# Gate and up products of three feed-forward stages by seven products of quarters

## The chip, the cores and the metric

The kernel runs on one core of a Trainium2 chip. The metric is device time in microseconds of one execution. Every engine (TensorE for matmuls, VectorE, ScalarE, GpSimd, SyncE) works through its own queue in order; semaphores tie the queues together. In the profile TensorE is PE (PEld: its weight loads), VectorE DVE, ScalarE ACT, GpSimd POOL, SyncE SP.

## The reference

Two transformer blocks over 512 tokens of 1024 float32 values. The first (attention, convolution and a mixture of experts) is not touched. The second has two layers; each has a feed-forward stage, a mixer (a pooling mixer in layer 0, MLA, a latent attention, in layer 1) and a second feed-forward stage:

```python
def swiglu(h, w_gate, w_up, w_down):
    return (jax.nn.silu(h @ w_gate) * (h @ w_up)) @ w_down
...
    for i in range(DEPTH_2):
        h = rmsnorm_2(x, ffn1_norm[i])
        x = x + FFN_HALF * swiglu(h, ffn1_w_gate[i], ffn1_w_up[i], ffn1_w_down[i])
        h = rmsnorm_2(x, mix_norm[i])
        ...
        h = rmsnorm_2(x, ffn2_norm[i])
        x = x + FFN_HALF * swiglu(h, ffn2_w_gate[i], ffn2_w_up[i], ffn2_w_down[i])
```

Gate and up are 1024 x 2816, down is 2816 x 1024. Below FFN(1,0), FFN(2,0), FFN(1,1) and FFN(2,1) are the four stages in order of time (first or second of a layer, layer); the pooling mixer stands between the first two, MLA between the last two.

## The kernel before

**Products.** A float32 product is made of three matmuls (`mm3`, L247 to L249): each operand is split into a high part (`hi`, a cast on ScalarE) and a low part (`lo`, the rest, a subtraction on VectorE), and hi x hi, hi x lo and lo x hi add up in PSUM. Stationary is a 128x128 tile of weights, moving are the tokens (transposed, `xT`, hidden values on partitions), 512 columns at a time.

**Weights.** `Weights` holds the whole program's list of weight units. SyncE fetches raw chunks of 1 MB into a ring (`wraw`); `_split` makes `whi` (L161, ScalarE) and `wlo` (L162, VectorE) of a unit of at most 128x1024. `next` hands the next unit to the products and splits ahead, two units beyond the one in use, into rings of `NU` = 4 buffers.

**A feed-forward stage** (`ffn`). A front norms the 512 tokens (X, float32, in four groups of 128): square sum on ScalarE (`junk`, L275), root on GpSimd, product `hrow` on VectorE (L282), eight transposes on TensorE into `pB` and `pC` (L294), cast `xTh` (L255) and split `xTl` (L256). The hidden width is done in 22 blocks of 128 columns, in three parts, `PARTS` = (0,8), (8,15), (15,22). A block is a gate product (24 matmuls of 512 columns: 8 slices of 1024 times 3) into one half of a two-bank PSUM tile `pA`, an up product into its other half, Silu on ScalarE (L1052), product of both on VectorE (L1054), and the split of that into `hh` (L255) and `hl` (L256). The first two blocks run on tokens 0 to 255 first and on 256 to 511 afterwards, so that TensorE can begin when two of four token groups are normed. After each part come the down products of its blocks, for the two halves of the output columns (`dh`): four accumulators, one per token group, in `pB` and `pC`, and at the end X is updated (L1103). In the last part the second half runs token group by token group, so that the next stage's front can begin with the first. There are two `pA` tiles of two banks, two `pB` and two `pC` of one bank.

**Order.** A scheduler sets the order of each engine's queue from the order of the code and from priorities (the front runs with a raised one), when the program is built. PSUM and SBUF tiles are guarded as whole tiles: an instruction that writes one half of a `pA` tile waits for a reader of the other half that comes before it in the code.

## Time and profile before

| | us |
|---|---|
| median of 3 runs (2659.57 to 2660.88) | 2659.93 |
| the profiled execution | 2662.16 |
| its span in the trace | 2660.4 |
| TensorE busy | 2554.8 (96%) |
| VectorE busy | 1046.5 (39%) |
| ScalarE busy | 735.2 (28%) |

The stages in the trace: projections, attention and experts up to about 820 us, FFN(1,0) to 1215, pooling mixer to 1244, FFN(2,0) to 1622, FFN(1,1) to 2005, MLA to 2280, FFN(2,1) to 2656. Records of matmuls overlap, since the next starts while the former drains through the array: the time from start to start is what one costs in a stream, and a window's count of matmuls gives the same. Records of weight loads lie under the matmuls. The granted clock (PEclk) is a share of full speed.

### The profile page before, as it was taken

The numbers are of one execution on the slowest core, as the hardware profiler recorded it, in microseconds if no ns is written. First come the engines' busy times: TensorE is split into PE (matmuls) and PEld (weight loads), VectorE is DVE, ScalarE is ACT, GpSimd is POOL, SyncE is SP. The second block draws the span as 40 slices with busy tenths as digits, with TensorE's granted clock in tenths as the row PEclk, the third lists the DMA queues.
The fourth block names the chain that finished last, engine by engine and source line by source line (L and its number), as shares of the span: only waits on it lengthen the run. The fifth ranks groups of instructions, "written<-read, shape, count | busy, mean of one in ns | idle before, by whom it ended". The sixth has DMA issues, their size and how long they took to land.

```text
span 2660.4 us, 28926 instructions
## 1 busy us (share of the span) xinstructions
PE 2554.8 (96%) x12006; PEld 1858.5 (70%) x12006; DVE 1046.5 (39%) x1627; ACT 735.2 (28%) x1243; POOL 90.9 (3%) x142
## 2 busy tenths in 40 slices
PE   6999889999998999998999999999999999999999
PEld 4855644333335887888887878777778777888887
DVE  5665322222225333336333334333335566533332
ACT  4333210000003322224322223222224645322221
POOL 1000200000001000001000000000001000000000
PEclk9999889999998999999999999999999999999999
DMA  7254479999996323232232322223222111122321
GB/s 266 92 178 166 164 290 420 408 416 419 418 419 217 104 87 97 86 103 83 95 96 87 94 98 94 95 79 103 79 87 80 58 58 64 64 99 76 119 76 59
DMA packets 185492, 411.90 MB, mean 155 GB/s; under 512 B 7460, under 2 KB 126784, under 8 KB 157712
## 3 DMA queue, kind: packets, MB, share of 16 engines
q1 hardware_dynamic: 183168, 403.73, 41.5%
q0 software_dynamic: 1184, 2.97, 0.3%
q10 hardware_dynamic: 1008, 3.34, 0.3%
q8 instruction: 94, 1.54, 0.2%
q14 instruction: 38, 0.31, 0.0%
HBM read 407.92 MB, written 2.10 MB: 154 GB/s over the span
## 4 chain that ended last, share of the span: by engine, by line
PE 61%; issue 30%; DVE 3%; ACT 3%; DMA 2%; POOL 2%; SPq 0%; ACTq 0%; POOLq 0%; DVEq 0%
PE pA L966 9%; PE pA L247 7%; PE pA L248 7%; PE pA L249 7%; PE pB L966 4%; PE pC L248 3%; PE pC L249 3%; PE pC L247 3%; PE pB L248 2%; PE pB L247 2%; PE pB L249 2%; PE pC L940 1%; PE ms L1397 1%; PE pC L1015 1%; PE pC L741 1%
## 5 line engine op out<-in xcount | busy, mean ns | idle before, releaser
L161 ACT CAST whi<-wraw 128x1024 fp32r<-128x1024 f32 (+2 forms) x334 | 335.9, 1011 | 1092.1 <-PE pA L248 684.8
L162 DVE TENSOR_TENSOR wlo<-wraw,whi 128x1024 fp32r<-128x1024 f32 (+2 forms) x334 | 391.9, 1177 | 479.6 <-ACT whi L161 468.1
L248 PE MATMUL pA<-xTl,whi 128*128 128x512 f32 (+1 forms) x1536 | 578.1, 377 | 1.3 <-DVE xTl L256 1.3
L249 PE MATMUL pA<-xTh,wlo 128*128 128x512 f32 (+1 forms) x1536 | 578.0, 377 | 0.0
L247 PE MATMUL pA<-xTh,whi 128*128 128x512 f32 (+1 forms) x1536 | 574.1, 381 | 3.4 <-ACT xTh L255 3.0
L247 PEld LDWEIGHTS pA<-xTh,whi 128*128 128x128 f32 x1536 | 289.7, 189 | 78.9 <-ACT sl L1052 21.9
L249 PEld LDWEIGHTS pA<-xTh,wlo 128*128 128x128 f32 x1536 | 289.8, 189 | 56.7
L248 PEld LDWEIGHTS pA<-xTl,whi 128*128 128x128 f32 x1536 | 290.2, 189 | 54.7 <-DVE xTl L256 1.7
L1054 DVE TENSOR_TENSOR sl<-pA,sl 128x512 f32<-128x512 f32 x88 | 60.9, 692 | 427.6 <-PE pA L249 427.5
L966 PE MATMUL pA<-wraw,wideh 128*64 128x512 f32 x832 | 215.9, 597 | 0.5 <-DVE wideh L949 0.5
L966 PEld LDWEIGHTS pA<-wraw,wideh 128*64 128x64 f32 x832 | 63.4, 137 | 109.3 <-issue 108.2
L247 PE MATMUL pC<-whi,hh 128*128 128x512 f32 x352 | 138.5, 393 | 0.0
L248 PE MATMUL pC<-wlo,hh 128*128 128x512 f32 x352 | 138.5, 393 | 0.0
L249 PE MATMUL pC<-whi,hl 128*128 128x512 f32 x352 | 138.4, 393 | 0.0
L247 PE MATMUL pB<-whi,hh 128*128 128x512 f32 x352 | 138.3, 393 | 0.0
L248 PE MATMUL pB<-wlo,hh 128*128 128x512 f32 x352 | 138.3, 393 | 0.0
L249 PE MATMUL pB<-whi,hl 128*128 128x512 f32 x352 | 138.1, 392 | 0.0
L966 PE MATMUL pB<-wraw,hx 128*64 128x512 f32 x320 | 100.5, 596 | 0.0
L262 POOL TENSOR_SCALAR ms<-ss 128x1 f32<-128x1 f32 x46 | 18.8, 409 | 1747.1 <-ACT junk L275 1713.5
L247 PEld LDWEIGHTS pB<-whi,hh 128*128 128x128 f32 x352 | 66.1, 188 | 15.5 <-DVE X L1103 0.7
L247 PEld LDWEIGHTS pC<-whi,hh 128*128 128x128 f32 x352 | 66.1, 188 | 14.9
L249 PEld LDWEIGHTS pB<-whi,hl 128*128 128x128 f32 x352 | 66.1, 188 | 14.8
(495 smaller groups left out, 3314.5 us busy)
## 6 DMA issues: line engine op xcount, KB each, us to landing
wraw<-in_w_up_dram SPq DMA_DIRECT2D x61, 1024.0 KB, 12.4
wraw<-in_w_gate_dram SPq DMA_DIRECT2D x43, 1024.0 KB, 12.0
wraw<-in_w_down_dram SPq DMA_DIRECT2D x40, 1024.0 KB, 10.5
wraw<-in_ffn_w_gate_dram SPq DMA_DIRECT2D x40, 1024.0 KB, 5.3
wraw<-in_ffn_w_up_dram SPq DMA_DIRECT2D x40, 1024.0 KB, 5.3
wraw<-in_ffn_w_down_dram SPq DMA_DIRECT2D x32, 1024.0 KB, 4.9
wraw<-in_w_ada_dram SPq DMA_DIRECT2D x24, 1024.0 KB, 7.8
widel<-in_w_down_dram SPq DMA_DIRECT2D x16, 1024.0 KB, 7.7
```

What stands on the lines that cost most here:

```text
L161: self.nc.scalar.copy(out=hi, in_=src)
L162: self.nc.vector.tensor_sub(lo, src, f(hi))
L247: PE.matmul(o, a[0], b[0], start=first, stop=False)
L248: PE.matmul(o, a[0], b[1], start=False, stop=False)
L249: PE.matmul(o, a[1], b[0], start=False, stop=last)
L262: G.tensor_scalar(ms, ss, 1.0 / n, EPS, op0=OP.mult, op1=OP.add)
L741: PE.matmul(o[r], Vf[:, blk, r], x, start=z == 0, stop=z == len(blks) - 1)
L940: PE.matmul(p, ohr[:, t], h[:, t, c_], start=t + z == 0, stop=t + z == T)
L966: PE.matmul(outs[dh][r], x[:, k, r], ws[e][:, j, dh * 512:(dh + 1) * 512], start=k == 0, stop=k == K - 1)
L1015: PE.matmul(p, Se[:, t * P:(t + 1) * P], ys[dh][s], start=s == 0, stop=s == 1)
L1054: V.tensor_mul(sl, a[:, 512:1024], sl)
L1397: PE.matmul(p[:, :nn], q[a][:, c_], k[b][:, :nn], start=first, stop=False)
```

## The change

`ffn_fast` takes the place of `ffn` in FFN(2,0), FFN(1,1) and FFN(2,1). The hidden width is done in 11 pairs of 256 columns, in four parts, `PAIRS`. A gate or up product of a pair is a product of 256 columns x 1024 by 1024 x 512 tokens; cut into quarters (256 in two halves of 128, 1024 in two of 512, tokens in two of 256) it is eight products of 12 matmuls of 256 tokens as it stands, and seven with sums of quarters (Winograd's form of Strassen's method). `seven` picks where: gates from pair 2, ups of pair 1 and of even pairs. The other products stay 2 x 24 matmuls of 512.

For a product by seven, `sums` puts four units in the list instead of two. `_form` makes the sums of weight quarters on VectorE (four operations of 512), and three units of 1024 and one of 512 are split. The sums of token quarters are made once in each stage by `form_sums`, from a float32 copy of the tokens (`x32`) that ScalarE writes in the front beside `xTh`. The seven results are put together on VectorE (three operations of 512 and one of 256: L1214, L1218, L1219, L1223 of the changed kernel) and a copy of 256 on ScalarE (L1210). A gate by seven takes both `pA` tiles, an up by seven the two `pB` and two `pC`; the down products of dh = 0 take `pA` tiles. Silu, the product, and the split of the hidden values act on 1024 elements at a time. `mla_tables`, which runs on the small engines inside FFN(2,0), shares some of its tiles.

```diff
@@ -119,6 +119,26 @@
+    def sums(self, c):
+        self.units.append((c, lambda v: v[:, :, 0:P], 0))
+        self.units.append((c, 0, 0))
+        self.units.append((c, 1, 0))
+        self.units.append((c, lambda v: v[:, 4:8, P:2 * P], 0))
+        self.left[c] += 4
+    def _form(self, v, which):
+        a11, a12, a21, a22 = v[:, 0:4, 0:P], v[:, 4:8, 0:P], v[:, 0:4, P:2 * P], v[:, 4:8, P:2 * P]
+        t = self.tmp.tile([P, 1024], F32, name="wsum", tag="wsum", bufs=2).rearrange("p (a b) -> p a b", b=P)
+        if which == 0:
+            self.nc.vector.tensor_add(t[:, 4:8], a21, a22)
+            self.nc.vector.tensor_sub(t[:, 0:4], t[:, 4:8], a11)
+            self.second = t[:, 0:4]
+        else:
+            self.nc.vector.tensor_sub(t[:, 0:4], a11, a21)
+            self.nc.vector.tensor_sub(t[:, 4:8], a12, self.second)
+        return t
@@ -151,7 +171,7 @@
     def _split(self, i):
         c, pick, raw = self.units[i]
-        src = pick(self.tiles[c])
+        src = self._form(self.tiles[c], pick) if isinstance(pick, int) else pick(self.tiles[c])
@@ -387,7 +407,30 @@
     PARTS = [(0, 8), (8, 15), (15, 22)]
+    PAIRS = [(0, 3), (3, 6), (6, 9), (9, 11)]
+    def seven(pr, m):
+        return pr > 1 and (m == 0 or pr % 2 == 0) or pr == 1 and m == 1
+    def plan_fast(which, i):
+        g, u, d = (I[f"ffn{which}_w_{n}_2"][i] for n in ("gate", "up", "down"))
+        for p0, p1 in PAIRS:
+            for pr in range(p0, p1):
+                for m, ap in enumerate((g, u)):
+                    c = W.chunk([(0, P, rows(ap, 0, K, 2 * pr * P, 2 * P))], (P, K, 2 * P))
+                    if seven(pr, m):
+                        W.sums(c)
+                        continue
+                    for a in range(2):
+                        W.unit(c, lambda v, a=a: v[:, :, a * P:(a + 1) * P])
+            for dh in range(2):
+                plan_cols(d[2 * p0 * P:2 * p1 * P], 2 * (p1 - p0), dh * 512, 512, 4, 2)
     def plan_ffn(which, i):
+        if (which, i) != (1, 0):
+            plan_fast(which, i)
+            return
         g, u, d = (I[f"ffn{which}_w_{n}_2"][i] for n in ("gate", "up", "down"))
@@ -1104,6 +1147,148 @@
+    def ffn_fast(pool, gain, last=False, hook=None):
+        W.tmp = pool
+        xT = pair()
+        st = ExitStack()
+        xp = st.enter_context(tc.tile_pool(name="x32", reuse_waits=RW, bufs=1))
+        x32 = xp.tile([P, K, S], F32, name="x32")
+        def put_at(t):
+            two = split_into(xT, t)
+            def put(g, m, pv):
+                two(g, m, pv)
+                A.copy(out=x32[:, g:g + m, t * P:(t + 1) * P], in_=pv)
+            return put
+        with tc.high_priority(offset=200):
+            for t in range(T):
+                transposed(norm_rows(nrms[1], X[:, t], gain), K, put_at(t))
+        nrms[0].close()
+        right = ExitStack()
+        tp = right.enter_context(tc.tile_pool(name="tsum", reuse_waits=RW, bufs=1, side="right"))
+        ts = [tp.tile([P, 4, 4, 256], F32R, name="ts" + z) for z in "hl"]
+        def form_sums():
+            b11, b12, b21, b22 = (x32[:, a:a + 4, c:c + 256] for a in (0, 4) for c in (0, 256))
+            t = [xp.tile([P, 4, 256], F32, name=n, tag=n) for n in ("tsa", "tsb")]
+            def done(i, v):
+                split(ts[0][:, i], ts[1][:, i], v)
+            V.tensor_sub(t[0], b12, b11)
+            V.tensor_sub(t[1], b22, t[0])
+            done(1, t[1])
+            done(0, t[0])
+            V.tensor_sub(t[0], b22, b12)
+            done(2, t[0])
+            V.tensor_sub(t[1], b21, t[1])
+            done(3, t[1])
+        def proj(o, w, c0, c1):
+            for k in range(K):
+                mm3(o[:, c0:c1], [x[:, k] for x in w], [x[:, k, c0:c1] for x in xT], k == 0, k == K - 1)
+        def product(o, w, k0, b):
+            for k in range(4):
+                mm3(o, [x[:, k0 + k] for x in w], [x[:, k] for x in b], k == 0, k == 3)
+        def plain(k0, c0):
+            return [x[:, k0:k0 + 4, c0:c0 + 256] for x in xT]
+        def by_seven(bk, res):
+            two = [b.rearrange("p (h n) -> p h n", h=2) for b in bk]
+            tt = [[x[:, i] for x in ts] for i in range(4)]
+            w = W.next()
+            product(two[3][:, 0], w, 0, plain(0, 0))
+            m1 = pool.tile([P, 256], F32, name="m1", tag="m1", bufs=1)
+            A.copy(out=m1, in_=two[3][:, 0])
+            product(two[0][:, 0], w, 4, plain(4, 0))
+            w = W.next()
+            product(two[0][:, 1], w, 0, tt[1])
+            V.tensor_add(res[:, 0::3], two[0], m1[:, None, :].to_broadcast([P, 2, 256]))
+            product(two[1][:, 0], w, 4, tt[0])
+            w = W.next()
+            product(two[1][:, 1], w, 0, tt[2])
+            V.tensor_add(res[:, 1:3], two[1], res[:, 3:4].to_broadcast([P, 2, 256]))
+            V.tensor_add(res[:, 3], two[1][:, 0], res[:, 2])
+            product(two[2][:, 0], w, 4, plain(4, 256))
+            w = W.next()
+            product(two[2][:, 1], w, 0, tt[3])
+            V.tensor_add(res[:, 1:3], two[2], res[:, 1:3])
+        hp = None
+        for p0, p1 in PAIRS:
+            if hook is not None and p0 > 0:
+                hook()
+                hook = None
+            hs = []
+            for pr in range(p0, p1):
+                ga = [psA(), psA()] if seven(pr, 0) else [psA()]
+                ub = [psB(), psB(), psC(), psC()] if seven(pr, 1) else [psB(), psC()]
+                gb = [a[:, c:c + 512] for a in ga for c in (0, 512)]
+                rg = pool.tile([P, 4, 256], F32, name="rg", tag="rg", bufs=1)
+                rgf = rg.rearrange("p a n -> p (a n)")
+                if pr == 0:
+                    ws = []
+                    for o in gb + ub:
+                        ws.append(W.next())
+                        proj(o, ws[-1], 0, 256)
+                    form_sums()
+                    st.close()
+                    hp = st.enter_context(tc.tile_pool(name="hid", reuse_waits=RW, bufs=3))
+                    for o, w in zip(gb, ws):
+                        proj(o, w, 256, 512)
+                elif seven(pr, 0):
+                    by_seven(gb, rg)
+                else:
+                    for o in gb:
+                        proj(o, W.next(), 0, 512)
+                A.activation(rgf, rgf if seven(pr, 0) else ga[0], AF.Silu)
+                if seven(pr, 1):
+                    ru = pool.tile([P, 4, 256], F32, name="ru", tag="ru", bufs=1)
+                    by_seven(ub, ru)
+                    V.tensor_mul(rgf, ru.rearrange("p a n -> p (a n)"), rgf)
+                else:
+                    for j, o in enumerate(ub):
+                        if pr == 0:
+                            proj(o, ws[2 + j], 256, 512)
+                        else:
+                            proj(o, W.next(), 0, 512)
+                        V.tensor_mul(rgf[:, j * 512:(j + 1) * 512], o, rgf[:, j * 512:(j + 1) * 512])
+                hh, hl = (hp.tile([P, 1024], F32R, name=n, tag=n) for n in ("hh", "hl"))
+                split(hh, hl, rgf)
+                hs.append((hh, hl))
+            n = 2 * (p1 - p0)
+            for dh in range(2):
+                a = [psA(), psA()] if dh == 0 else None
+                acc = [x[:, c:c + 512] for x in a for c in (0, 512)] if a else [psB(), psB(), psC(), psC()]
+                c_ = slice(dh * 512, (dh + 1) * 512)
+                if dh == 1 and 2 * p1 == FB:
+                    ws = [W.next() for _ in range(n // 2)]
+                    order = [(t, z) for t in range(T) for z in range(n)]
+                else:
+                    ws = []
+                    order = [(t, z) for z in range(n) for t in range(T)]
+                for t, z in order:
+                    if z // 2 == len(ws):
+                        ws.append(W.next())
+                    h0 = z % 2 * 512 + t * P
+                    mm3(acc[t], [x[:, h0:h0 + P] for x in hs[z // 2]], [x[:, z % 2] for x in ws[z // 2]],
+                        z == 0, z == n - 1)
+                    if z == n - 1:
+                        V.scalar_tensor_tensor(X[:, t, c_], acc[t], 0.5, X[:, t, c_], op0=OP.mult, op1=OP.add)
+        st.close()
+        right.close()
+        open_nrm()
...
@@ -1488,13 +1673,13 @@
         with tc.tile_pool(name="f20", reuse_waits=RW, bufs=1) as p_:
             nxt, gain = gain, load_gain(I["ffn1_norm_2"][1:2])
             mcs = []
-            ffn(p_, nxt, hook=lambda: mcs.extend(mla_tables(ml)))
+            ffn_fast(p_, nxt, hook=lambda: mcs.extend(mla_tables(ml)))
             nxt, gain = gain, load_gain(I["mix_norm_2"][1:2])
-            ffn(p_, nxt)
+            ffn_fast(p_, nxt)
-        ffn(p_, gain, last=True)
+        ffn_fast(p_, gain, last=True)
```

TensorE's queue in the second part of FFN(2,0). Before, where the up of block 10 begins (`pA_8498` is its tile, `pA_8566` that of block 11):

```order
L249 MATMUL pA_8566<-xTh_7338,wlo_8501 128x512
L247 MATMUL pA_8566<-xTh_7338,whi_8500 128x512
L247 MATMUL pA_8498<-xTh_7338,whi_8465 128x512 [waits Activation_49]
L248 MATMUL pA_8498<-xTl_7339,whi_8465 128x512
L249 MATMUL pA_8498<-xTh_7338,wlo_8466 128x512
```

After, in the gate of pair 4 (`pA_8556` holds its first two sums, `pA_8557` the other two; `whi_8523`, `whi_8566` and `whi_8596` are its second, third and fourth unit):

```order
L268 MATMUL pA_8557<-xTl_7341,whi_8566 128x256
L269 MATMUL pA_8557<-xTh_7340,wlo_8567 128x256
L267 MATMUL pA_8557<-tsh_7450,whi_8596 128x256
L267 MATMUL pA_8556<-tsh_7450,whi_8523 128x256 [waits DVE_49]
L268 MATMUL pA_8556<-tsl_7451,whi_8523 128x256
L269 MATMUL pA_8556<-tsh_7450,wlo_8524 128x256
```

Seven matmuls of the block behind, of which the last two are shown, stood in front of a wait on ScalarE's Silu. Now a whole product of the third unit and one matmul of the fourth stand in front of a wait on VectorE, inside a gate.

VectorE's queue at the same place; before, two blocks (`sl` is the product with the gate, `hl` the low part of the hidden values):

```order
L162 TENSOR_TENSOR wlo_8437<-wraw_8154,whi_8436 128x1024 [waits DMAHW0_49,PE_49,Activation_49]
L1054 TENSOR_TENSOR sl_8367<-pA_8366,sl_8367 128x512 [waits PE_49,Activation_49]
L162 TENSOR_TENSOR wlo_8466<-wraw_8220,whi_8465 128x1024 [waits DMAHW1_49,Activation_49]
L256 TENSOR_TENSOR hl_8431<-sl_8367,hh_8430 128x512 [waits Activation_49]
L162 TENSOR_TENSOR wlo_8501<-wraw_8154,whi_8500 128x1024 [waits PE_49,Activation_49]
L1054 TENSOR_TENSOR sl_8435<-pA_8434,sl_8435 128x512 [waits PE_49,Activation_49]
L162 TENSOR_TENSOR wlo_8532<-wraw_8220,whi_8531 128x1024 [waits Activation_49]
L256 TENSOR_TENSOR hl_8495<-sl_8435,hh_8494 128x512 [waits Activation_49]
```

After, the gate of pair 4 by seven (`hl_8553` belongs to pair 3, `rg` is the gate's result, `ru` the up's):

```order
L276 TENSOR_TENSOR hl_8553<-rg_8376,hh_8552 128x1024 [waits Activation_49]
L182 TENSOR_TENSOR wlo_8628<-wraw_8224,whi_8627 128x1024 [waits PE_49,Activation_49]
L1214 TENSOR_TENSOR rg_8562<-pA_8556,m1_8582 128x2x256 [waits DVE_49,PE_49]
L182 TENSOR_TENSOR wlo_8661<-wsum_8657,whi_8660 128x1024 [waits PE_49,Activation_49]
L1218 TENSOR_TENSOR rg_8562<-pA_8556,rg_8562 128x512 [waits DVE_49,PE_49]
L182 TENSOR_TENSOR wlo_8683<-wsum_8679,whi_8682 128x1024 [waits Activation_49]
L1219 TENSOR_TENSOR rg_8562<-pA_8556,rg_8562 128x256 [waits DVE_49]
L182 TENSOR_TENSOR wlo_8713<-wraw_8224,whi_8712 128x512 [waits PE_49,Activation_49]
L1223 TENSOR_TENSOR rg_8562<-pA_8557,rg_8562 128x512 [waits DVE_49]
L134 TENSOR_TENSOR wsum_8773<-wraw_8414 128x512 [waits DMAHW0_49]
L138 TENSOR_TENSOR wsum_8803<-wraw_8414 128x512
L182 TENSOR_TENSOR wlo_8744<-wraw_8414,whi_8743 128x1024 [waits PE_49,Activation_49]
```

Before, two splits of weights and two operations on hidden values take turns; now the result sums that wait on TensorE stand between splits of the units for the next products, and the forms of weights (`wsum`) are added.

ScalarE's queue at the front of FFN(1,1), from the first square sum. Before:

```order
L275 ACTIVATE junk_9746,ss_9747<-X_71 128x1024 [waits DVE_49,Pool_49]
L255 CAST xTh_9744<-pB_9755 128x4x128 [waits PE_49]
L275 ACTIVATE junk_9769,ss_9770<-X_71 128x1024 [waits DVE_49,Activation_49,Pool_49]
L255 CAST xTh_9744<-pB_9778 128x4x128 [waits PE_49]
L275 ACTIVATE junk_9792,ss_9793<-X_71 128x1024 [waits DVE_49,Activation_49,Pool_49]
L255 CAST xTh_9744<-pC_9762 128x4x128 [waits PE_49]
L161 CAST whi_9646<-wraw_9489 128x1024 [waits DMAHW6_49,PE_49]
L161 CAST whi_9650<-wraw_9556 128x1024 [waits DMAHW7_49,PE_49]
L255 CAST xTh_9744<-pB_9801 128x4x128 [waits PE_49]
L255 CAST xTh_9744<-pC_9785 128x4x128 [waits PE_49]
```

After (`x32` is the float32 copy):

```order
L295 ACTIVATE junk_10598,ss_10599<-X_71 128x1024 [waits DVE_49,Pool_49]
L295 ACTIVATE junk_10623,ss_10624<-X_71 128x1024 [waits DVE_49,Activation_49,Pool_49]
L275 CAST xTh_10592<-pB_10607 128x4x128 [waits PE_49]
L181 CAST whi_10708<-wraw_10374 128x1024 [waits DMAHW7_49,PE_49]
L275 CAST xTh_10592<-pB_10632 128x4x128 [waits PE_49]
L295 ACTIVATE junk_10648,ss_10649<-X_71 128x1024 [waits DVE_49,Activation_49,Pool_49]
L1165 COPY x32_10597<-pB_10607 128x4x128 [waits PE_49]
L275 CAST xTh_10592<-pC_10615 128x4x128
L1165 COPY x32_10597<-pB_10632 128x4x128 [waits DVE_49]
L181 CAST whi_10736<-wraw_10374 128x1024 [waits PE_49]
L1165 COPY x32_10597<-pC_10615 128x4x128 [waits DVE_49]
L275 CAST xTh_10592<-pB_10657 128x4x128 [waits PE_49]
```

The copies of `x32` stand between the casts `xTh`; each frees the PSUM tile of a transpose later than the casts alone did.

## Rows read from the trace of the kernel before

**Rows 1.** Page, part 1: busy time, share of the span, count of instructions.
```profile
PE 2554.8 (96%) x12006; PEld 1858.5 (70%) x12006; DVE 1046.5 (39%) x1627; ACT 735.2 (28%) x1243; POOL 90.9 (3%) x142
```

**Rows 2.** Windows in two feed-forward stages; columns in the first line.
```profile
core 0: us, PE busy (x) PEld busy (x) DVE busy (x) ACT busy (x) POOL busy (x), PEclk, DMA share, GB/s
...
1300.00:1350.00 50.00, 50.00 (x215) 39.89 (x215) 15.42 (x17) 13.23 (x16) 0.00 (x0) 1.00 0.27 91
1400.00:1450.00 50.00, 50.00 (x214) 39.66 (x213) 16.20 (x17) 13.62 (x18) 0.00 (x0) 1.00 0.28 95
```

**Rows 3.** Waits of TensorE, 2285 to 2660: total us, times, longest.
```profile
PE pB L294 <- DVE xTl L256: 1.0, 1, 1.0
```

**Rows 4.** Timeline of TensorE: start, duration, line, tiles, shapes; one place in consecutive blocks.
```profile
1400.74 0.73 PE L247 MATMUL pA<-xTh,whi 128*128 128x512 f32 x2
...
1411.99 0.71 PE L247 MATMUL pA<-xTh,whi 128*128 128x512 f32 x2
```

**Rows 5.** Timeline of TensorE in the halves of 256 tokens, 15 matmuls.
```profile
1253.73 0.28 PE L247 MATMUL pA<-xTh,whi 128*128 128x256 f32 x1
...
1255.39 0.28 PE L249 MATMUL pA<-xTh,wlo 128*128 128x256 f32 x1
```

**Rows 6.** Groups by line and shape: count, busy us, mean ns, idle before.
```profile
L162 DVE TENSOR_TENSOR wlo<-wraw,whi 128x1024 fp32r<-128x1024 f32 x294 | 358.8, 1224 | 461.6 <-ACT whi L161 450.3 <-PE pB L623 4.1
L161 ACT CAST whi<-wraw 128x1024 fp32r<-128x1024 f32 x294 | 306.7, 1048 | 1009.6 <-PE pA L248 639.2 <-PE pC L249 284.5 <-issue 24.4
...
L247 PEld LDWEIGHTS pA<-xTh,whi 128*128 128x128 f32 x1536 | 289.7, 189 | 78.9 <-ACT sl L1052 21.9 <-ACT xTh L255 3.9
...
L1054 DVE TENSOR_TENSOR sl<-pA,sl 128x512 f32<-128x512 f32 x88 | 60.9, 692 | 427.6 <-PE pA L249 427.5
L256 DVE TENSOR_TENSOR hl<-sl,hh 128x512 fp32r<-128x512 f32 x88 | 60.3, 685 | 0.7
L255 ACT CAST hh<-sl 128x512 fp32r<-128x512 f32 x88 | 54.7, 621 | 3.3 <-DVE sl L1054 3.3
...
L162 DVE TENSOR_TENSOR wlo<-wraw,whi 128x512 fp32r<-128x512 f32 x16 | 10.9, 680 | 0.0
```

**Rows 7.** Timeline of VectorE: back to back (1228), then inside a block (1418).
```profile
1229.63 0.68 DVE L256 TENSOR_TENSOR pll<-pB,plh 128x512 fp32r<-128x512 f32 x1
1230.22 1.28 DVE L256 TENSOR_TENSOR pll<-pC,plh 128x512 fp32r<-128x512 f32 x2
1231.42 0.68 DVE L1157 TENSOR_TENSOR X<-pB,X 128x512 f32<-128x512 f32 x1
...
1418.18 0.69 DVE L1054 TENSOR_TENSOR sl<-pA,sl 128x512 f32<-128x512 f32 x1 [5.26 <-PE pA L249]
1418.96 1.23 DVE L162 TENSOR_TENSOR wlo<-wraw,whi 128x1024 fp32r<-128x1024 f32 x1
1420.10 0.68 DVE L256 TENSOR_TENSOR hl<-sl,hh 128x512 fp32r<-128x512 f32 x1
```

**Rows 8.** Waits of TensorE in the whole run, the one on a Silu.
```profile
PE pA L247 <- ACT sl L1052: 0.2, 1, 0.2
```

**Rows 9.** Timelines, front of FFN(1,1): VectorE's X sum and norm, TensorE's transposes.
```profile
1610.09 0.68 DVE L1103 SCALAR_TENSOR_TENSOR X<-pB,X 128x512 f32<-128x512 f32 x1
1612.98 1.28 DVE L282 SCALAR_TENSOR_TENSOR hrow<-X,rstd,gain 128x1024 f32<-128x1024 f32 x1 [2.21 <-POOL rstd L263]
...
1614.41 0.63 PE L294 MATMUL pB<-cst,hrow 128*128 128x128 f32 x4 [0.69 <-DVE hrow L282]
```

**Rows 10.** Waits of TensorE, 1600 to 1650.
```profile
PE pB L294 <- DVE hrow L282: 2.3, 4, 0.7
```

**Rows 11.** Windows ahead of FFN(2,1), columns as in rows 2.
```profile
2284.00:2286.00 2.00, 1.09 (x6) 1.12 (x7) 2.00 (x5) 1.01 (x2) 0.74 (x2) 0.74 1.03 347
2286.00:2288.00 2.00, 2.00 (x11) 2.00 (x11) 2.00 (x3) 1.17 (x2) 0.00 (x0) 0.50 0.31 102
```

More of the change, by code (lines that the diff above doesn't have):

```diff
@@ L1105, in ffn @@
                             nc.sync.dma_start(out=out[0, t * P:(t + 1) * P, c_], in_=X[:, t, c_])
+    def ffn_fast(pool, gain, last=False, hook=None):
[119 more added lines that the diff above has]
+                        V.scalar_tensor_tensor(X[:, t, c_], acc[t], 0.5, X[:, t, c_], op0=OP.mult, op1=OP.add)
+                        if last and 2 * p1 == FB:
+                            nc.sync.dma_start(out=out[0, t * P:(t + 1) * P, c_], in_=X[:, t, c_])
+        st.close()
+        right.close()
+        open_nrm()
@@ L1171, in mla_tables @@
             V.tensor_scalar(ang[:, t], cst[:, C_INV:C_INV + 32], pos[:, t:t + 1], None, op0=OP.mult)
-        cs = lp.tile([P, T, 32], F32, name="cs")
+        cs = ang
         sn = lp.tile([P, T, 2, 32], F32, name="sn")
-        for o, q, off in ((cs, 0.25, TWO_PI / 4), (sn[:, :, 1], 0.0, 0.0)):
-            n = lp.tile([P, T, 32], F32, name="nturn", tag="nturn", bufs=2)
-            r = lp.tile([P, T, 32], F32, name="rang", tag="rang", bufs=2)
+        for o, q, off in ((sn[:, :, 1], 0.0, 0.0), (cs, 0.25, TWO_PI / 4)):
+            n = lp.tile([P, T, 32], F32, name="nturn", tag="nturn")
+            r = lp.tile([P, T, 32], F32, name="rang", tag="rang")
             V.tensor_scalar(n, ang, 1.0 / TWO_PI, q, op0=OP.mult, op1=OP.add)
@@ L1198, in mla_tables @@
         gcol = pool.tile([P, 1], F32, name="gcolqk")
-        gqk = lp.tile([P, NOPE], F32, name="gqk")
+        gqk = lp.tile([P, NOPE], F32, name="gqk", tag="rang")
         V.tensor_mul(gqk, gqh[:, 0:NOPE], gkh[:, 0:NOPE])
```

## The prediction

> **What bounds the kernel now.** I read the page's busy shares first. TensorE is busy for 96% of the span, and it loads weights once per matmul [rows 1]. A share alone does not say that an engine is full, so next come the windows inside a feed-forward stage. In 50 us TensorE is busy for all 50, with 214 or 215 matmuls, that is 0.2326 us from one to the next at a granted clock of 1.00. VectorE is busy for 15 to 16 us of the 50 and ScalarE for 13 to 14 [rows 2]. Last come the waits of TensorE: in the final stage, 375 us long, the one wait listed is 1.0 us [rows 3]. So these stages last as long as their matmuls take, and VectorE has two thirds of its time free. A stage starts with a front that is bound otherwise (norm, transposes), below.
>
> **What the change removes.** A block of 128 hidden columns (gate and up, 48 matmuls of 512 tokens) takes 1411.99 - 1400.74 = 11.25 us from one block's place to the same place in the next [rows 4]; 48 x 0.2326 is 11.16, so 0.09 of it is stall. A gate or up matrix of a pair (256 columns) is the same 48 matmuls. Seven products of 12 matmuls of 256 tokens replace them: 84. Such matmuls stand in the trace of before, where the first two blocks are done in halves: 14 pitches from 1253.73 to 1255.39 make 0.1186 us each [rows 5]. 84 x 0.1186 = 9.96 us. The gain is 1.29 us for each matrix. The rule `seven` picks 9 gates (pairs 2 to 10) and 6 ups (1, 2, 4, 6, 8, 10), so 15 in a stage, 45 in three: **58.0 us**, if TensorE never waits longer than now. The order of the changed kernel shows the 84 matmuls per matrix, so that the change does nothing is excluded.
>
> A rule speaks against this step. The Trainium skill (page "TensorE: Matmul & The Clock Gate", section "Back-to-back issue gap") gives, for a real stream of loads and matmuls, about 81 ns at 128 columns and 131 ns at 512, because the load is part of the spacing. Between them, an estimate from that page for 256 columns is 98 ns: 84 x 98 = 8.2 us against 48 x 131 = 6.3 us, a loss of 1.9 us per matrix, 87 us in all. The trace does not agree: its ratio of the two pitches is 0.51, not 0.75.
>
> **What it adds on VectorE.** Durations: a split of 1024 elements 1.224 us, of 512 0.680, an operation of 512 with a PSUM operand 0.692 [rows 6]. One matrix by seven needs 4 weight sums of 512 (4 x 0.685 = 2.74), splits (3 x 1.224 + 0.68 = 4.35), result sums, three of 512 and one of 256 (the splits of 1024 and 512 lie 0.544 apart, so 256 is 0.27 below 512, 0.41): 2.07 + 0.41 = 2.48. Together 9.57 us. Then come the product with the gate and the split of the hidden values, two operations of 1024 per pair. A pair with both by seven asks 2 x 9.57 + 2.45 = 21.6 us of VectorE in 2 x 9.96 = 19.9 us of TensorE; a pair with the gate only asks some 14.6 in 21.2, and the down products ask little. Back to back VectorE does better than its durations: a 512 starts every 0.60 us, a 1024 every 1.14 [rows 7], which makes 7 x 0.60 + 0.60 + 3 x 1.14 + 0.33 = 8.55 for 9.57, and 19.4 for 21.6. So it fits on average, with the pairs of both kinds alternating, and the splits, which run two units ahead (24 x 0.1186 = 2.8 us each), carry a heavy pair. VectorE goes from a third to nearly nine tenths busy: its cover is gone, and what it does in its order begins to count. ScalarE gets three casts of 1024 at 1.05, one of 512 at 0.62 [rows 6] and a copy of 256 per matrix, about 4.1 us of 9.96, and stays free.
>
> **Stalls inside a gate (cost).** The two accumulators of a gate pair share one two-bank tile, and the order shows a wait on VectorE before the second product of the second sum. It waits for the first result sum (L1214), because that reads the other half of the tile. The order puts 13 matmuls of other products ahead (23 in gates 2, 5 and 7): 13 x 0.1186 = 1.54 us of cover. Needed: 0.16 us (a 256 record lasts 0.28 and is followed after 0.12 [rows 5]), a hop, and 0.69 for the sum, some 0.93, plus what VectorE is in the middle of, 0 to 1.22. So a wait of 0 to 0.6; going through the order with the durations I get 0.15 in six gates and 0.25 to 0.5 in the three where the hidden split (1.22) stands in front of the sum. Per stage 6 x 0.15 + 3 x 0.4 = 2.1 us, **6 us** in three (bounds 1 and 25). The nearest row is the same guard today, 7 matmuls ahead of the up of a block (1.63 us) against a Silu on ScalarE: 0.2 us in the whole run [rows 8], but there the waited-for engine is idle. Behind that wait on TensorE stands everything, since its matmuls stay in order. The ups use four tiles and have no such wait.
>
> **Fronts (cost).** From the last sum into X of a 128-token group to its transposes it takes 1614.41 - 1610.09 = 4.32 us [rows 9]. Today the last down runs group by group, 7 x 3 x 0.2326 = 4.88 us each, and hides that: TensorE waits 2.3 us there in all [rows 10]. The last part now has 4 blocks: 4 x 3 x 0.2326 = 2.79 us a group, so after the second group there are 5.6 us of cover instead of 9.8 for a chain of 4.32 plus transposes 0.6, cast 0.62 and split 0.68, about 6.2 us: 1 us more with what is queued there. Then ScalarE copies the tokens in float32 (8 x 0.6 = 4.8 us), in order with the casts that the first products wait for; about half of it falls ahead of the last one, 2.4 us. This front (into the second fast stage) gets +3.5. The front of MLA behind that stage gets the shorter cover alone, +1.5; the fronts of the first and the last fast stage get the copies alone, and part of them is hidden, +1 and +1.5. Together **7.5 us** (bounds 1 and 16). The token sums (8 x 1.14 = 9.1 us on VectorE) run under the second halves, 4 x 24 x 0.1186 = 11.4 us: nothing, if they start on time.
>
> **Parts (cost).** Down dh=0 now accumulates in two-bank tiles. At its end the second half waits for the X add of the first: 0.24 + 0.69 less 3 matmuls (0.70), about 0.2 us, at 12 ends: **2.5 us** (0 to 6). Weight bytes, DMA issues and the last output are unchanged, and the table changes of MLA stand off the path.
>
> **Sum.** 58.0 - 6 - 7.5 - 2.5 = 42 us. The profiled execution took 2662.16 us (span 2660.4), 2.2 above the median: 2620.2 there, **2618 us** beside the median of 2659.9. By the bounds of the costs it is 2604 to 2649.
>
> **Rivals.**
> - The guards all hold as they do now: only some 4 us of fronts are lost, 2606. For it speaks that VectorE's pitch is below its duration [rows 7]; against it that gates with the hidden split in front exist.
> - VectorE is short in the heavy pairs. By durations, plus 0.09 us between each of its 26 operations (as from 1418.18 + 0.69 to 1418.96 [rows 7]), a pair asks 23.9 us against 19.9; 15 such pairs, half of it absorbed by the light pair behind: 15 x 2.0 = 30 us more, 2648. The Trainium skill has this as a rule (page "VectorE: DVE Perf Modes", section "The DRAIN you can't avoid"): the next operation does not start until the pipe is empty. The trace does not agree for independent operations: 0.60 us between starts where one lasts 0.68.
> - Slower: VectorE becomes the bound, because it works in order. If each of the three result sums that wait for a product holds VectorE for 1 us while splits for the next units stand behind it, a matrix takes 9.57 + 3.0 = 12.6 us instead of 11.25: +1.3 x 45 = 60 us, 2720. It decides from 42 / 45 = 0.93 us of further stall per matrix, that is from a matrix of some 11.1 us. For it: the order puts a split between any two result sums, and result sums wait on TensorE. Against it: the look-ahead of two units.
> - Slower by the pitch: the load records last 0.189 us [rows 6] and would bind if they did not overlap, 84 x 0.189 = 15.9 us a matrix, 4.6 x 45 = 209 us more and 16 of stalls, 2885; it decides from a pitch of 0.130 (42 us over 45 x 84 matmuls are 0.011). The pitch of 0.1186 in rows 5 speaks against it. This is the mechanism of the Trainium skill's rule above ("Back-to-back issue gap").
> - A stage front idles so long that the clock drops, as now ahead of the last stage, where the clock is 0.74 and 0.50 and 11 matmuls pass in 2 us instead of 17 [rows 11]: 0.7 us for each such 2 us; with three such windows at each of four fronts 8 us, 2626.
>
> **How the numbers follow.** Chances: my sum 0.55, guards as now 0.15, clock at the fronts 0.05, heavy pairs short 0.13, VectorE bound 0.09, pitch 0.03. A measurement tells about 0.2% (5 us) from no change. The first three are faster, and so is most of the fourth (0.11): 0.86. Of the fourth and fifth 0.04 lie within 0.2%, and 0.10 are slower. The range of 8 in 10 leaves out those, and the outer ends of the second and fourth: 2600 to 2652.
>
> **What would show it.** Right: in the three stages some 420 matmuls of 256 columns per 50 us in the sevens, VectorE at 80 to 90% there, TensorE's waits for L1214 of about 0.15 to 0.5 us and 6 in sum, fronts of 4 to 6 us. Each of the three stages is about 14 us shorter. Wrong: TensorE waiting for wlo of L182 or ScalarE's whi inside the pairs (VectorE bound); a pitch above 0.13; waits for L1214 near 1 us; fronts idle over 10 us.

## The result

2611.71 us (median of 4 runs, 2610.74 to 2612.97) against 2660.4 for the kernel before on the same chip: ratio 0.9823, 95% interval 0.9809 to 0.9837. The forecast was 2618, range 2600 to 2652. The span of the profiled execution is 2611.2 us, 49.2 less.

The page of the changed kernel, parts 1 and 2 (busy time; tenths busy in 40 slices), beside [rows 1]:

```profile
PE 2502.4 (96%) x13626; PEld 1907.4 (73%) x13626; DVE 1374.8 (53%) x2068; ACT 844.6 (32%) x1342; POOL 90.8 (3%) x142
...
PE   6999979999997999999999999999999999999999
...
DVE  5655332222215333335866767666665666767665
```

TensorE has 1620 matmuls more and 52 us less of work; VectorE has 328 us more, nearly all in the three stages (the last 20 slices or so), and TensorE's row stays at 9 there. Windows in pairs of FFN(2,0), columns as in [rows 2]:

```profile
1350.00:1400.00 50.00, 49.90 (x362) 46.93 (x361) 36.60 (x46) 21.59 (x24) 0.00 (x0) 1.00 0.29 93
1450.00:1500.00 50.00, 50.00 (x376) 47.70 (x376) 39.80 (x51) 23.58 (x28) 0.00 (x0) 1.00 0.26 85
```

VectorE works for 37 to 40 us of 50 instead of 15 to 16, and TensorE is still busy for 49.9 and 50.0. The durations are those of before: the split of a weight form, the first result sum, a matmul of a token sum (groups by line and shape):

```profile
L182 DVE TENSOR_TENSOR wlo<-wsum,whi 128x1024 fp32r<-128x1024 f32 x90 | 110.0, 1222 | 109.8 <-ACT whi L181 109.0
...
L269 PE MATMUL pA<-tsh,wlo 128*128 128x256 f32 x432 | 120.3, 282 | 0.0
...
L1214 DVE TENSOR_TENSOR rg<-pA,m 128x512 f32<-128x512 f32 x27 | 18.5, 684 | 0.3
```

**Where the time went.** The start times of TensorE's matmuls in the traces cut the end of the program into four: each stage from its first projection matmul to the next stage's (FFN(1,1) and FFN(2,1) to their last down matmul; MLA is what lies between these two). All in us, one profiled execution each; "from start" is the sum of the four (differences in the text are taken before rounding):

| kernel | first matmul of FFN(2,0) | FFN(2,0) | FFN(1,1) | MLA | FFN(2,1) | from start |
|---|---|---|---|---|---|---|
| before | 1244.1 | 379.0 | 377.0 | 283.4 | 372.4 | 1411.8 |
| after | 1244.0 | 360.7 | 364.7 | 280.8 | 356.6 | 1362.8 |
| e1, no seven | 1242.4 | 377.2 | 378.1 | 280.7 | 371.5 | 1407.5 |
| e2, gates only | 1242.1 | 368.4 | 368.6 | 281.7 | 363.8 | 1382.5 |
| e3, all pairs | 1240.0 | 355.2 | 359.9 | 280.6 | 351.2 | 1346.8 |
| e4, banks | 1242.7 | 359.4 | 364.4 | 281.7 | 356.2 | 1361.7 |
| e5, no copies | 1244.0 | 359.7 | 361.4 | 280.5 | 356.6 | 1358.1 |
| e6, parts | 1241.1 | 360.8 | 361.9 | 278.2 | 357.4 | 1358.3 |
| e7, doubled sums | 1241.6 | 361.3 | 364.3 | 280.5 | 357.2 | 1363.3 |
| e8, all pairs, doubled | 1244.9 | 360.2 | 364.0 | 281.1 | 356.7 | 1362.1 |
| e9, joined | 1245.0 | 355.4 | 357.3 | 278.2 | 352.7 | 1343.6 |
| e10, joined, pair 1 | 1242.6 | 354.4 | 355.9 | 281.1 | 351.9 | 1343.2 |
| e11, joined, GpSimd | 1244.0 | 358.7 | 361.5 | 280.0 | 350.5 | 1350.7 |
| e12, after again | 1241.4 | 360.5 | 363.6 | 280.5 | 356.5 | 1361.1 |

The first column tells how far a whole time can be trusted: up to the front of FFN(2,0) the program is the same in all of them, and it varies by 5 us. Below, differences of a few us are taken from the stages, not from the medians. They have an error too: the changed kernel and e12, which is the same kernel, differ by 1.6 us from start. A part of it is the clock. From the first matmul of FFN(2,0) on, TensorE's granted clock was at 0.50 (1.2 instead of 2.4 GHz) for 13.7 us in the trace of before, 10.2 of them in MLA, for 10.2 us in that of the changed kernel, and for 3.4 us in e1 and in e12.

### The profile page after: what moved, and what is told of

Its sections match the earlier page's. It is cut to its first block, busy times and chain, and to the rows that moved or that the text cites. A ratio compares the mean times of both kernels' runs of the same rounds, so it can differ in the third digit from the quotient of the medians.

```text
span 2611.2 us, 32928 instructions
## 1 busy us (share of the span) xinstructions
PE 2502.4 (96%) x13626; PEld 1907.4 (73%) x13626; DVE 1374.8 (53%) x2068; ACT 844.6 (32%) x1342; POOL 90.8 (3%) x142
## 4 chain that ended last, share of the span: by engine, by line
PE 60%; issue 30%; DVE 3%; ACT 3%; DMA 2%; POOL 2%; SPq 0%; POOLq 0%; ACTq 0%; DVEq 0%
PE pA L1009 9%; PE pA L267 5%; PE pA L269 5%; PE pA L268 5%; PE pB L1009 4%; PE pC L268 3%; PE pC L269 3%; PE pC L267 3%; PE pB L268 3%; PE pB L269 3%; PE pB L267 3%; PE pC L983 1%; PE ms L1582 1%; DMA wraw<-in_w_ada_dram 1%; PE pC L1058 1%
## 5 line engine op out<-in xcount | busy, mean ns | idle before, releaser
L268 PE MATMUL pA<-xTl,whi 128*128 128x256 f32 (+1 forms) x852 | 283.5, 333 | 4.2 <-DVE xTl L276 4.2
L267 PE MATMUL pA<-xTh,whi 128*128 128x256 f32 (+1 forms) x852 | 282.3, 335 | 4.5 <-ACT xTh L275 3.9
L269 PE MATMUL pA<-xTh,wlo 128*128 128x256 f32 (+1 forms) x852 | 283.4, 333 | 0.0
L267 PEld LDWEIGHTS pA<-xTh,whi 128*128 128x128 f32 x852 | 161.5, 190 | 27.1 <-ACT sl L1095 6.0
L268 PEld LDWEIGHTS pA<-xTl,whi 128*128 128x128 f32 x852 | 161.9, 190 | 21.4 <-DVE xTl L276 5.3
L269 PEld LDWEIGHTS pA<-xTh,wlo 128*128 128x128 f32 x852 | 161.9, 190 | 16.3
L182 DVE TENSOR_TENSOR wlo<-wsum,whi 128x1024 fp32r<-128x1024 f32 x90 | 110.0, 1222 | 109.8 <-ACT whi L181 109.0
L267 PE MATMUL pA<-tsh,whi 128*128 128x256 f32 x432 | 122.4, 287 | 0.3
L268 PE MATMUL pA<-tsl,whi 128*128 128x256 f32 x432 | 120.7, 281 | 0.0
L269 PE MATMUL pA<-tsh,wlo 128*128 128x256 f32 x432 | 120.3, 282 | 0.0
```

What stands on the lines that cost most here:

```text
L182: self.nc.vector.tensor_sub(lo, src, f(hi))
L267: PE.matmul(o, a[0], b[0], start=first, stop=False)
L268: PE.matmul(o, a[0], b[1], start=False, stop=False)
L269: PE.matmul(o, a[1], b[0], start=False, stop=last)
```

## The experiments

**e1, e2, e3: how many products by seven.**

```diff
     def seven(pr, m):
-        return pr > 1 and (m == 0 or pr % 2 == 0) or pr == 1 and m == 1
+        return False
```

That is e1; e2 has `pr > 1 and m == 0` there, e3 `pr > 1 or pr == 1 and m == 1`.

> The changed kernel with no product by seven at all: the pairs, the four parts, the float32 copies in the front, the token sums and the two-bank accumulators of the down products stay, and every gate and up is done in matmuls of 512. Theory A (the gain is the arithmetic of the products, 1.29 us a matrix less small stalls, and the rest of the change only costs): slower than the kernel before by the fronts and parts, 2660.4 + 5 to 10 = 2666 to 2670. Theory B (a part of the 49 us comes from something else, such as the units in pairs or the fronts): at or below the kernel before, 2655 to 2660.

> Products by seven in the gates of pairs 2 to 10 alone, 27 matrices instead of 45, so no pair has both. Theory A: 18 x (1.29 - 0.05) = 22 us slower than the changed kernel, 2634. Theory C (VectorE is short in the heavy pairs, so that the ups there gain little or nothing): the same as the changed kernel within 5 us, 2607 to 2617.

> Products by seven in gate and up of every pair from 2 on, and the up of pair 1: 19 a stage, 57 in all, all pairs heavy for VectorE. Theory A with VectorE at its pitch (19.4 us of work in 19.9 us): 12 x 1.29 = 15 us less than the changed kernel, 2596, VectorE nearly full. Theory C (a heavy pair asks 21.6 to 23.9 us by durations and lives on the light pair behind it, which is now gone): 27 heavy pairs short by 1.7 to 4 us each, 2640 to 2700.

Measured: e1 2657.08 us, ratio to before 0.9996 (0.9987 to 1.0006); e2 2630.83, 0.9897 (0.9883 to 0.9912); e3 2596.70, 0.9771 (0.9752 to 0.9791). From start, against e1: 27 gates give 25.0 us (0.93 each), 18 ups 19.7 more (1.10 each), the 12 ups of odd pairs 15.9 more (1.33 each). Theory C, a shortage in heavy pairs, falls: the ups that make a pair heavy gain no less than the gates. Theory A holds for the products, but not for the rest of the change: without them it costs nothing in whole times. It is 4.3 us faster from start, 2.7 of it in MLA, but its clock was low for 10.2 us less, which at half speed is worth up to 5.1 us. So that the rest is a gain (theory B, whose 2655 to 2660 was hit) is not shown. e3's windows in pairs that are all heavy:

```profile
1345.00:1395.00 50.00, 50.00 (x420) 49.83 (x420) 44.93 (x59) 24.56 (x29) 0.00 (x0) 1.00 0.28 93
1440.00:1490.00 50.00, 50.00 (x421) 49.83 (x420) 45.71 (x60) 24.59 (x30) 0.00 (x0) 1.00 0.27 88
```

420 matmuls in 50 us, 0.1190 us each: all time goes into products. VectorE shows 59 records where 26 operations in each 20 us pair make 65; some records are missing, so it is busier than the 90% shown. Its list shows how it keeps up:

```profile
1445.60 0.68 DVE L1218 TENSOR_TENSOR rg<-pA,rg 128x512 f32<-128x512 f32 x1
1446.20 1.21 DVE L182 TENSOR_TENSOR wlo<-wsum,whi 128x1024 fp32r<-128x1024 f32 x1
1447.33 0.42 DVE L1219 TENSOR_TENSOR rg<-pA,rg 128x256 f32<-128x256 f32 x1
1447.66 0.68 DVE L182 TENSOR_TENSOR wlo<-wraw,whi 128x512 fp32r<-128x512 f32 x1
1448.26 0.68 DVE L1223 TENSOR_TENSOR rg<-pA,rg 128x512 f32<-128x512 f32 x1
1448.87 0.68 DVE L134 TENSOR_TENSOR wsum<-wraw 128x512 f32<-128x512 f32 x1
```

An operation of 512 starts 0.60 us, one of 1024 1.13 us, one of 256 0.33 us ahead of the next, each while the former still runs. By starts a heavy pair asks 19.4 us, by durations 21.6, and it has 20.0.

**e7, e8: where VectorE becomes the bound.** The first two result sums of each product are done twice:

```diff
             V.tensor_add(res[:, 0::3], two[0], m1[:, None, :].to_broadcast([P, 2, 256]))
+            V.tensor_add(res[:, 0::3], two[0], m1[:, None, :].to_broadcast([P, 2, 256]))
...
             V.tensor_add(res[:, 1:3], two[1], res[:, 3:4].to_broadcast([P, 2, 256]))
+            V.tensor_add(res[:, 1:3], two[1], res[:, 3:4].to_broadcast([P, 2, 256]))
```

> The changed kernel with the first two result sums of each product by seven done twice, 90 operations of 512 more on VectorE, 54 us of its time by starts of 0.60. A pair of both kinds then asks 2 x 9.75 + 2.28 = 21.8 us of VectorE in 19.9 of TensorE, the pair behind it 14 in 21. Theory A2 (the splits that run two units ahead, up to 5.7 us, carry a pair that is 1.9 us short): within 5 us of the changed kernel, 2612 to 2617. Theory C2 (a sum that comes late is paid by TensorE at once): 15 x 1.9 = 28 us more, 2640.

> The same doubled sums with products by seven in every pair from 2 on: 114 operations more, and every pair asks 21.8 us of VectorE in 19.9 of TensorE. Theory A2: the splits ahead and the down products cover the first pairs of a part only; 27 pairs short by 1.9 us are 51, less up to 5.7 us at the head of each of 12 parts: 10 to 40 us above the same kernel without doubling (2597), so 2607 to 2637. If VectorE never binds, 2597.

Measured: e7 2612.97 us, 0.983 (0.9816 to 0.9845), 0.5 us from start above the changed kernel: 54 us of added work for nothing. e8 2611.34, 0.9823 (0.9808 to 0.9838), 15.3 us from start above e3. So one heavy pair that is 1.9 us short is carried by the splits ahead and the light pair behind it; in a row they are not. (In e8 too the first pair of a part loses nothing, with 20.3 us as in e3.) A window of e8, then the waits of TensorE's weight loads and of ScalarE on weight units, from 1250 us on:

```profile
1345.00:1395.00 50.00, 48.90 (x393) 47.35 (x392) 44.45 (x63) 21.72 (x27) 0.00 (x0) 1.00 0.23 74
```

```profile
PEld pC L267 <- ACT whi L181: 7.0, 6, 1.2
...
PEld pA L269 <- DVE wlo L182: 3.3, 13, 0.3
...
PEld pC L269 <- DVE wlo L182: 3.1, 15, 0.2
```

```profile
ACT whi L181 <- DVE wsum L135: 77.4, 24, 4.1
```

This is the slower rival at work: 393 matmuls instead of 420, and TensorE waits for `wlo`, and for `whi`, whose cast on ScalarE waits for a weight sum of VectorE (77.4 us in all, 9.7 in the changed kernel). Three pairs take 62.8 to 62.9 us instead of 60.1 to 60.3. The bound thus lies between 19.4 and 21.8 us of VectorE's starts per pair of 19.9.

**e4: the wait inside a gate.**

```diff
-                gb = [a[:, c:c + 512] for a in ga for c in (0, 512)]
+                gb = [a[:, c:c + 512] for c in (0, 512) for a in ga]
```

> The changed kernel with the accumulators of a gate by seven dealt to the two pA tiles in turn, so that the tile of the second sum is not the one whose first half the first result sum reads; the order then has 24 matmuls between that sum's products and the first matmul that waits for it, instead of 13. Theory D (the 1.4 us a stage seen behind the early matmul are the wait for the sum): 4 us less, 2608. Theory E (a wait that stands in the middle of a stream costs TensorE some 0.1 us even when it is long met, as the up of each block shows in the kernel before): 1 to 2 us less, 2610.

Measured: 2612.48 us, 0.9828 (0.9812 to 0.9845), no difference in whole times. What the edit takes away stands in the changed kernel's timelines, VectorE and TensorE in a gate with the hidden split in front:

```profile
1392.61 1.22 DVE L276 TENSOR_TENSOR hl<-rg,hh 128x1024 fp32r<-128x1024 f32 x1
1393.93 0.69 DVE L1214 TENSOR_TENSOR rg<-pA,m 128x512 f32<-128x512 f32 x1
```

```profile
1394.29 0.28 PE L268 MATMUL pA<-tsl,whi 128*128 128x256 f32 x1
1394.68 0.39 PE L267 MATMUL pA<-tsh,whi 128*128 128x256 f32 x1
1394.90 0.28 PE L268 MATMUL pA<-tsl,whi 128*128 128x256 f32 x1
```

The sum ends at 1394.62, TensorE goes on at 1394.68 instead of 1394.41: 0.27 us, and 0.10 more behind the waiting matmul. In e4 the parts 2 to 4 of the three stages are 1.3, 0.7 and 0.3 us shorter, 2.3 in all. That is not the whole of the stalls, since e4 still has the wait, behind 24 matmuls instead of 13. The start times give them: a gate by seven of the changed kernel takes 10.13 to 10.35 us where the order keeps it in one piece, an up by seven, which has no such wait, 9.96 to 9.97. An up and the gate behind it, 9.97 and 10.34 us from start to start:

```profile
1377.44 0.28 PE L267 MATMUL pC<-xTh,whi 128*128 128x256 f32 x1
...
1387.41 0.28 PE L267 MATMUL pA<-xTh,whi 128*128 128x256 f32 x1
...
1397.75 0.40 PE L267 MATMUL pB<-xTh,whi 128*128 128x512 f32 x1
```

Summed over the matmuls in gates by seven, what their pitch exceeds 0.1186 is 5.2 us in the changed kernel and 2.3 in e4. Theory D named the right wait; its 4 us and the 1 to 2 us of theory E lie on either side of the 2.3 to 2.9 us that the edit takes away, and whole times do not resolve that.

**e5, e6: the fronts.**

e5:

```diff
-                A.copy(out=x32[:, g:g + m, t * P:(t + 1) * P], in_=pv)
...
-            b11, b12, b21, b22 = (x32[:, a:a + 4, c:c + 256] for a in (0, 4) for c in (0, 256))
+            b11, b12, b21, b22 = (f(xT[0][:, a:a + 4, c:c + 256]) for a in (0, 4) for c in (0, 256))
```

e6:

```diff
-    PAIRS = [(0, 3), (3, 6), (6, 9), (9, 11)]
+    PAIRS = [(0, 2), (2, 5), (5, 8), (8, 11)]
```

> The changed kernel without the eight float32 copies of the tokens on ScalarE in each front; the token sums are made from the high parts of the tokens alone, so the low parts are left out of them. Theory F (the copies hold back the casts that the first products wait for, at all three fronts): 5 us less than the changed kernel, 2607, with the first part of the second fast stage some 2.5 us shorter. Theory G (the front loses by the shorter cover of the last part, and the copies lie beside other work): within 1 us of the changed kernel, 2611 to 2613.

> The changed kernel with the parts (0,2), (2,5), (5,8), (8,11), so that the last part has 6 blocks and each token group of its second half takes 4.19 us on TensorE instead of 2.79; the first part has 4. Theory G: the two fronts behind a last part (second fast stage, MLA) wait 1 to 2 us less each, 2608 to 2610. Theory F: no difference, 2611 to 2613.

Measured: e5 2607.06 us, 0.9805 (0.9789 to 0.9821); e6 2606.13, 0.9803 (0.9789 to 0.9818). Both gain some 4.5 us from start (some 3 against e12, whose clock fell less often), so neither F nor G is excluded: without the copies FFN(2,0) and FFN(1,1) are shorter by 1.0 and 3.3 us, with the longer last part FFN(1,1) and MLA by 2.8 and 2.6. TensorE's waits at the front of FFN(1,1) in the changed kernel (1595 to 1632), then in e5 and in e6:

```profile
PE pB L314 <- DVE hrow L302: 2.9, 4, 1.4
PE pA L267 <- ACT xTh L275: 0.9, 1, 0.9
PE pC L314 <- ACT x L1165: 0.4, 1, 0.4
PE pA L268 <- DVE xTl L276: 0.3, 1, 0.3
```

```profile
PE pB L314 <- DVE hrow L302: 1.4, 3, 0.6
PE pA L268 <- DVE xTl L276: 0.6, 2, 0.3
```

```profile
PE pB L314 <- DVE hrow L302: 0.9, 2, 0.6
PE pA L268 <- DVE xTl L276: 0.8, 1, 0.8
PE pC L314 <- DVE X L1285: 0.3, 1, 0.3
```

The waits on the norm (`hrow`) and on a copy (`x`, L1165) are what the two edits shorten or end, and the clock falls behind them: in the changed kernel 10 matmuls pass in 1608 to 1612, then the clock stands at 0.63 on average.

```profile
1608.00:1612.00 4.00, 1.50 (x10) 1.06 (x10) 3.23 (x5) 3.15 (x7) 0.74 (x2) 0.95 0.39 109
1612.00:1616.00 4.00, 4.00 (x23) 4.00 (x24) 2.60 (x4) 2.40 (x5) 0.00 (x0) 0.63 0.82 286
```

In e5 the same 4 us (1608 to 1612) hold 28 matmuls, and the clock stays at 1.00. In e12, the changed kernel again, it stays too, with 13 matmuls in 1606 to 1610, and FFN(1,1) is 1.0 us shorter: the drop is not in every execution, and by this difference it costs about 1 us here.

**e9, e10, e11: joined.** e9 joins e3, e4 and e6. e10 gives the gate of pair 1 too (`return pr > 0`). e11 is e9 with

```diff
-                A.copy(out=x32[:, g:g + m, t * P:(t + 1) * P], in_=pv)
+                ix = (slice(None), slice(g, g + m), slice(t * P, (t + 1) * P))
+                G.tensor_add(x32[ix], f(xT[0][ix]), f(xT[1][ix]))
```

> Three edits joined: products by seven in every pair from 2 on (e3), the accumulators dealt in turn (e4), and the parts (0,2), (2,5), (5,8), (8,11) (e6). Theory (the three act at different places and add up): 2611.7 - 15 - 1 - 5 = 2591 by times scaled to the changed kernel's. If the longer last part only moves the load of VectorE together: 2596.

> The same with the gate of pair 1 by seven too, which needs the token sums one pair earlier and both pA tiles, one of which pair 0 still holds for its Silu. Theory H (the token sums and the Silu are done in time): 3 x 1.29 = 4 us less than the joined kernel. Theory I (TensorE waits for the sums or the tile in each first pair): no less, or up to 6 us more.

> The joined kernel of e9 with the float32 copies made on GpSimd, from the high and low parts of the tokens, instead of on ScalarE from PSUM. Theory F (the copies cost since they stand in ScalarE's order and hold PSUM tiles): up to 5 us less than the joined kernel, as without the copies. If the longer last part has taken that cost already, or GpSimd, which makes the roots of the norms too, is late with the last copies: no less, or up to 5 us more.

> The changed kernel itself, beside the three others on the same chip: 0.982 of the kernel before, and the measure of how well such ratios repeat.

Measured: e9 2595.45 us, 0.9762 (0.9746 to 0.9778); e10 2591.37, 0.9754 (0.9739 to 0.9768); e11 2601.09, 0.9789 (0.9774 to 0.9804); e12 2609.34, 0.9824 (0.9809 to 0.9838). From start e9 is 19.2 us below the changed kernel, e3 and e6 alone 15.9 and 4.4: they nearly add up. e10 takes 3.3 us more from the three stages (theory H, 4 expected) and loses 3.0 in MLA, which it does not touch; there its clock is low for 10.2 us, three times as long as in the changed kernel, and in e9 not at all. It beats both kernels, by 68.5 and 19.5 us from start, and e9 and e10 cannot be told apart by their intervals. In e11 the additions are too slow for the front, and stand in GpSimd's order ahead of a norm's root:

```profile
1602.65 8.30 POOL L1166 TENSOR_TENSOR x<-xTh,xTl 128x512 f32<-128x512 f32 x5 [3.25 <-PE pC L268]
1611.04 0.19 POOL L282 TENSOR_SCALAR ms<-ss 128x1 f32<-128x1 f32 x1
```

Five of them take 8.30 us, and TensorE then waits up to 5.5 us at once for the norm behind that root: 7.2 us lost from start.

## Why the prediction was right, and where its steps were off

The forecast of 42 us against 49 is right in sign, cause and range. Its terms come out near what the traces show; the 7 us between are an overlooked gain, three costs that were put a little or much too high, and the clock of the executions compared.

- **The products.** The pitch of 0.1186 carried over (0.1190 in e3), and with it the ratio 0.51 that stood against the figures of the Trainium skill for a stream of loads and matmuls ("TensorE: Matmul & The Clock Gate", "Back-to-back issue gap"). A matrix by seven without a wait takes 9.97 us against the 11.25 of before, so 1.29 was right, 58 us. In that are the 0.09 of a block's stall, which the pairs take away and not the sevens: a plain matrix of e1 needs 11.19 (its windows hold 216 and 217 matmuls in 50 us). So against e1 a matrix gains some 1.2, 54 us, and 49 less the stalls in gates. Measured are 44.8 from start: 16.5 us in FFN(2,0), which is all of it, 13.4 in FFN(1,1), 15.0 in FFN(2,1). What is missing stands in the first parts of these two, where the clock was low for 3.4 us each in the changed kernel and not in e1. In e12, without the drop, FFN(1,1) gains 14.5.
- **What was overlooked.** The stall of 0.09 was removed from the 45 matrices alone, but in pairs the up no longer writes the tile that Silu reads, so that plain pairs lose it as well: at five plain matrices of 512 columns a stage an estimate of 1.4 us by the pitches of before (some 1.8 us a stage in e1, where all are plain).
- **The front of MLA.** Put at +1.5; MLA came out shorter, by 2.6. An estimate from the clock accounts for that. The granted clock (third column from the end) in windows of MLA in before, the changed kernel, e9 and e10:

```profile
2050.00:2100.00 50.00, 44.11 (x220) 36.36 (x218) 27.53 (x63) 29.61 (x100) 7.50 (x12) 0.90 0.20 66
```

```profile
2019.00:2069.00 50.00, 44.47 (x249) 38.12 (x248) 30.02 (x69) 31.04 (x104) 7.32 (x12) 0.97 0.20 67
```

```profile
2000.00:2050.00 50.00, 43.96 (x257) 38.37 (x256) 30.18 (x63) 30.82 (x101) 8.72 (x13) 1.00 0.27 89
```

```profile
2000.00:2050.00 50.00, 44.98 (x231) 38.16 (x231) 28.65 (x64) 30.03 (x101) 7.50 (x12) 0.90 0.20 67
```

  e9 and e10 do the same work in MLA, and e10, low for 10.2 us, takes 3.0 us more. Before was low for 10.2 us as well: 283.4 less 3.0 is 280.4, what e3, e7 and e12 take without a drop (280.5 to 280.6). So by this estimate the front of MLA cost nothing, and the 2.6 us are luck: they come from which executions were compared. A longer last part does shorten MLA, by 2.3 us between e9 and e12, neither of which has a drop there.
- **The fronts with the products.** Idle time of TensorE there, by start times less pitches (0.1186 and 0.2333 us), is 1.5, 3.8 and 3.3 us before and 2.5, 7.9 and 4.5 after for FFN(2,0), FFN(1,1) and FFN(2,1): +1.0, +4.0 and +1.2, where 1, 3.5 and 1.5 were written. For FFN(1,1) the drop of the clock is in it (+2.8 in e12, without). But these costs are no sum of a copies' and a cover's share, as I had put it: e5 and e6 take back 3.3 and 2.8 us in FFN(1,1), so either edit ends nearly the whole wait. In FFN(2,1) e5 shows no gain, but its clock was low there for 6.8 us instead of 3.4, so what the copies cost there is not shown.
- **Stalls in gates.** 6 us, measured 5.2; the mechanism, and the 0.27 us where the hidden split stands in front, as described.
- **Parts.** 2.5 us was 0.2 at each of 12 ends. The stretches of 144 down matmuls take 33.71 us with their hand-over in FFN(2,0) and FFN(1,1); at 0.2333, the pitch that the down products had there before (185 matmuls in 43.17 us), they would take 33.60. So it is some 0.1 us at each end, 1.3 in all. (In FFN(2,1) the down products ran faster before and after, at 0.227 to 0.228; the record does not say why.) The list of the X add (L1285) of the changed kernel names who waits, 22 times:

```profile
  PEld pA L267: 5.0, 22
```

- **The sum.** 58 + 1.4 - 5.2 - 1.3 - 6.2 (fronts) + 2.6 (MLA) = 49, where 58 - 6 - 2.5 - 6 - 1.5 = 42 was written.
- **Rivals.** A VectorE bound by durations would have shown in e3: a heavy pair asks 21.6 us that way and is done in 20.0. I had taken half of what the Trainium skill says ("VectorE: DVE Perf Modes", "The DRAIN you can't avoid"): the same section adds that a next operation that is not held back starts earlier. The trace agrees with that, with 0.60 us between starts where one lasts 0.68. My chance of 0.13 on short pairs was too high by that; the bound is real, but starts later (e8). VectorE stood at 73 to 80% in the pairs, below the 80 to 90 forecast, because light pairs lie between. The clock fell at fronts, as one rival had it, but it was low for 10.2 us here and for 13.7 before, so it is no cost of the change.

## What to carry to other kernels

More but smaller matmuls pay where their pitch falls with their columns (0.2326 to 0.1186 us from 512 to 256), and here the trace of before had a stretch of the smaller size to read it from. Work added on another engine is to be counted by starts, not by durations, against the time of the stretch it lies in: at 97% of it nothing was lost, at 109% one short pair was carried by the splits ahead and the light pair behind it, and a row of them was not. Run the change without its core (e1): the side effects that were priced at 10 us cost nothing in whole times. And before a few us between two profiles are put down to the program, compare how long the clock was low in each.

## What was not expected of the hardware

A matmul behind one that waits started 0.10 us late, in the gates and, in the kernel before, behind the up's first matmul in each block: that was the 0.09 us of a block's stall. The drop of TensorE's clock at a front or in MLA comes in some executions of one kernel and not in others: in the changed kernel the clock fell behind 4 us with 10 matmuls (from 1608), in e12 there were 13 in such 4 us and it did not. In MLA e10, low for 10.2 us, was 3.0 us longer than e9, with no drop.
